# ScalarE issues the state space layer's row loads; its last group runs its steps in another order

## The chip, the cores and the metric

The kernel runs on one core of a Trainium2 chip. A core has five engines that work at the same time, each through its own list of instructions in a fixed order: TensorE (PE in the profile: matmuls and transposes), VectorE (DVE), ScalarE (ACT), GpSimd (POOL) and SyncE (SP). An instruction waits on semaphores for what it reads and for the buffer that it writes, and all that stands behind it on its engine waits with it. Transfers between the chip's memory and on-chip memory (DMA) are begun by an instruction of one of the engines and then run on 16 DMA engines; whoever needs the data waits for the landing. The metric is the time in microseconds (us) on the device.

## The reference

The program is a bidirectional encoder of two layers over 512 tokens of width 1024. Layer 0 mixes tokens with retention and neighbourhood attention, layer 1 with a state space mixer; each is followed by a gated feed-forward block with a short convolution, and all is normalised before and after. The change lies in the state space mixer:

```python
xbc = silu(depthwise_conv_centered(xbc, conv_w, conv_b))      # x, B, C of all groups
dt = softplus(dt_raw + dt_bias); log_a = dt * A               # per head and direction
# per group of 8 heads, chunks of 128 tokens:
seg = cs[:, :, None] - cs[:, None, :]                         # cs: running sums of log_a in a chunk
decay = exp(where(mask, seg, -inf))
y_intra = (q @ k^T * decay) @ v                               # within a chunk
y_inter = (q @ h) * exp(cs)                                   # from the state before the chunk
y = (y_fwd + y_bwd + x * d_skip) * silu(z)
yg = yg * rsqrt(mean(yg * yg) + EPS)                          # over the 512 channels of a group
out = (yg * norm_g) @ w_out
```

There are four groups of eight heads with 64 channels each. Every group has its own z, x, B and C projections (10 tiles of 128 channels) and its own 512 rows of `w_out`.

## The kernel before, in words

All large products are computed as three matmuls (`mm3`, L87 to L89): each operand is split into a rounded high part and a rest (`split`, L82 a cast on ACT, L83 a subtraction on DVE). A unit of weights (512 KB, `wst`) is loaded by SP, cast into `whi` on ACT, and its rest `wlo` made on DVE. So a matmul of 128x512 needs SP, ACT and DVE to have run ahead of PE.

`mixer1` is the state space mixer. It goes through the four groups, and for each through a string of steps, `SLOTS[g]`, which sets in which order the program is written; a scheduler then lays the instructions out per engine by their dependencies, priorities and free buffers. The steps are:

- `t6`: project tile 6 of this group, `n3`: project tile 3 of the next group (tile 0 is B, 1 is C, 2 to 5 are x, 6 to 9 are z). For tiles 0 to 5 a centred convolution of five taps follows (ACT L684, four DVE steps L687). `S` and `N`: SiLU of the waiting tiles of this or the next group (ACT, L693 and L696), and, for B and x, transposes on PE (L667) that ACT copies out (`bt`, `xt`, L668).
- `G`: the four products of C and B (`pg`, L712), copied to `gt` by ACT. `s0` to `s2`: the state after chunk 0 to 2 in both directions (PE `st` L723).
- `h3`: the decay matrix of head 3. Two rows of 512 running sums, one per direction, are loaded from the memory tensor `pd` and spread over all 128 partitions (tile `pb`, 256 KB each, L740, issued by SP). ACT adds a bias in eight pieces of 128x128 (L744), DVE merges the two directions (L746), ACT takes the exponential (`e`, L748), DVE multiplies by `gt` (L749).
- `i1`: the part of two heads (pair 1) that comes from the states: 6 PE products `pi` (L764), scaled on DVE by rows of `yd` that SP loads into `gain` (L756).
- `p1`: pair 1 itself: 8 PE products `py` from `e` and `xt` (L784), DVE adds `y` (L787) and multiplies by SiLU of z (L788), ACT squares (`sq`, L790), POOL adds the square to the sum of the group (L794), ACT and DVE split `y` into `yh` and `yl` (L796, L797).
- `r`: the mean of the squares by 4 products on PE (`pss`, L804), then DVE (L806) and POOL (`rg`, L808). `o0`, `o1`: the half-width output projections of the previous group (48 matmuls each), scaled by `rg` as they are added to `x`.

ACT needs a table for the exponential and another for SiLU; a change between them is an `ACT_TABLE_LOAD` row. After the last group the program (L889 to L899) multiplies its `y` by `w_out`: the two tiles of tokens 0 to 127 first (`first`), then `rms`, and then tile by tile the closing normalisation, and the norm and transposes (`pt`, L141) for the next block. All weights of that last projection are held at once, so that its eight halves need tiles from other tags: four from the states and four from `xt`.

Of the kernel before, what the change touches and what calls it, by code (L numbers as in the profile page):

```python
# [7 lines left out]
F32 = mybir.dt.float32  # L8
R32 = mybir.dt.float32r
BF16 = mybir.dt.bfloat16  # L10
U32 = mybir.dt.uint32
AF = mybir.ActivationFunctionType
ALU = mybir.AluOpType
# [3 lines left out]
P = 128  # L17
S = 512
NT = S // P
# [279 lines left out]
def mixer0(E, w0, w_v, w_fm, tabs, dist_d, logit, gn, bias, w_out, g_post_row, done):  # L299
# [235 lines left out]
NG = 4  # L535
HPG = 8
# [5 lines left out]
SLOTS = (  # L542
# [4 lines left out]
)  # L547


# [4 lines left out]
def mixer1(E, w_dt, w_fm, cw, dtc, cols, mask, w_out, g_post_row, done):  # L554
# [4 lines left out]
    nc, tc = E.nc, E.tc  # L559
    C = P  # L560
    H, H2 = SSD_H, 2 * SSD_H
    with ExitStack() as ctx:
        pool = lambda name, bufs: ctx.enter_context(tc.tile_pool(name=name, bufs=bufs))
        one, two, four = pool("m1", 1), pool("m1b", 2), pool("m1d", 4)
# [10 lines left out]
        mean = few.tile([P, 1], F32, name="mean")  # L575
# [9 lines left out]
        pd = E.dram.tile([H2, S], F32, name="pd")  # L585
# [84 lines left out]
        def project(o, i, ps=None):  # L670

            g = o["g"]
            if ps is None:
                w = E.wunit(w_fm[g, i])
                ps = E.mm.tile([P, S], F32, name="mm")
                E.proj_fm(ps, w)
            if i >= 6:
                r = four.tile([P, S], F32, name="z")
                o["silu"].append((r, ps, i))
                return  # L680
            r = (one if i == 0 else two if i == 1 else four).tile(
                [P, S], F32, name="bf" if i == 0 else "cf" if i == 1 else "xf")
            wc = lambda j: cwt[:, g, i, j:j + 1]
            nc.scalar.activation(r, ps, AF.Identity, scale=wc(2), bias=wc(5))  # L684
            for j, d in ((1, 1), (3, -1), (0, 2), (4, -2)):
                a, b = (slice(d, None), slice(0, S - d)) if d > 0 else (slice(0, S + d), slice(-d, None))
                nc.vector.scalar_tensor_tensor(r[:, a], ps[:, b], wc(j), r[:, a], op0=ALU.mult, op1=ALU.add)  # L687
            o["silu"].append((r, r, i))

        def silus(o):  # L690

            r, src, i = o["silu"][-1]
            lead = nc.scalar.activation(r, src, AF.Silu)  # L693
            with tc.issue_after(lead.ins):
                for r, src, _ in o["silu"][:-1]:
                    nc.scalar.activation(r, src, AF.Silu)  # L696
            for r, _, i in o["silu"]:
                o["t"][i] = r
                if i == 0:
                    o["bt"] = one.tile([P, NT, P], F32, name="bt")  # L700
                    to_tok(r, o["bt"])
                elif 2 <= i < 6:
                    if "x" not in o:
                        o["x"] = two.tile([P, NT, 512], F32, name="xt")
                    to_tok(r, o["x"][:, :, (i - 2) * P:(i - 1) * P])
            o["silu"] = []
# [9 lines left out]
        def state(o, dr, i):  # L716
# [14 lines left out]
                nc.vector.tensor_tensor(ns, ps, ns, op=ALU.add)  # L731
            o["st"][dr, i] = ns

        def head(o, j):

            g = o["g"]
            h = g * HPG + j
            pb = [three.tile([P, NT, C], F32, name="pb", bufs=5) for _ in range(2)]
            for dr in range(2):
                nc.sync.dma_start(pb[dr], pd[dr * H + h].partition_broadcast(P))  # L740

            for dr in range(2):
                for c in range(NT):
                    nc.scalar.activation(pb[dr][:, c], pb[dr][:, c], AF.Identity, scale=1.0 - 2 * dr,  # L744
                                         bias=tok[:, 0, c, dr * H + h:dr * H + h + 1])
            nc.vector.copy_predicated(pb[1], um.bitcast(U32).rearrange("p (o l) -> p o l", o=1).broadcast_to([P, NT, C]), pb[0])  # L746
            e = three.tile([P, NT, C], F32, name="e")
            nc.scalar.activation(e, pb[1], AF.Exp)  # L748
            o["m"][j] = e, nc.vector.tensor_tensor(e, e, o["gt"], op=ALU.mult)  # L749

        def inter(o, q):
# [24 lines left out]
        def pair(o, q):  # L776

            f = o["g"] * 4 + q
            y = o["yi"][q]
            py = E.px.tile([P, S], F32, name="py", tag="px")  # L780
            ms = [o["m"][2 * q + j] for j in range(2)]
            for c in range(NT):
                for j in range(2):
                    E.together([nc.tensor.matmul(py[j * 64:j * 64 + 64, c * C:(c + 1) * C],  # L784
                                                 o["x"][:, c, (2 * q + j) * 64:(2 * q + j + 1) * 64], ms[j][0][:, c],
                                                 start=True, stop=True)], [w for _, w in ms])
            nc.vector.tensor_tensor(y, py, y, op=ALU.add)  # L787
            nc.vector.tensor_tensor(y, y, o["t"][6 + q], op=ALU.mult)  # L788
            sq = (last if q == 0 else E.tmp).tile([P, S], F32, name="sq", tag="ssq" if q == 0 else "tmp")
            nc.scalar.activation(sq, y, AF.Square)  # L790
            if q == 0:
                o["sq"] = sq
            else:
                nc.gpsimd.tensor_tensor(o["sq"], o["sq"], sq, op=ALU.add)  # L794
            yh, yl = four.tile([P, S], R32, name="yh"), four.tile([P, S], R32, name="yl")
            nc.scalar.activation(yh, y, AF.Identity, scale=col[:, 1, f:f + 1])  # L796
            nc.vector.scalar_tensor_tensor(yl, y, col[:, 1, f:f + 1], yh.bitcast(F32), op0=ALU.mult, op1=ALU.subtract)  # L797
            o["y"].append((yh, yl))

        def rms(o):  # L800

            pss = E.px.tile([P, NT], F32, name="pss", tag="px")
            for c in range(NT):
                nc.tensor.matmul(pss[:, c:c + 1], o["sq"][:, c * C:(c + 1) * C], mean, start=True, stop=True)  # L804
            ss = few.tile([P, NT], F32, name="ss", bufs=2)
            nc.vector.tensor_scalar(ss, pss, EPS, None, op0=ALU.add)  # L806
            o["r"] = few.tile([P, NT], F32, name="rg", bufs=2)
            nc.gpsimd.tensor_tensor(o["r"], ss, E.mhalf.broadcast_to([P, NT]), op=ALU.pow)  # L808

        def out_mm(o, t, ws):  # L810
            ps = E.mm.tile([P, 512], F32, name="mm")
            tt = slice(t * P, (t + 1) * P)
            for k in range(4):
                yh, yl = o["y"][k]
                E.mm3(ps, yh[:, tt], yl[:, tt], *ws[k], k == 0, k == 3)
            return ps
# [19 lines left out]
            for t in range(NT):  # L836
                out_tile(o, n, t, ws)

        gs = [dict(g=g, t={}, st={}, m={}, yi={}, y=[], silu=[]) for g in range(NG)]
        def tiles(o, *ii):  # L840
            for i in ii:
                project(o, i)
            silus(o)

        w0 = [E.wunit(w_fm[0, i]) for i in range(3)]
        p0 = [E.mm.tile([P, S], F32, name="mm") for _ in range(3)]
# [6 lines left out]
            project(gs[0], i, p0[i])  # L853
        steps()
        three, ys, last = pool("m1e", 5), pool("m1y", 2), pool("m1f", 1)
        tiles(gs[0], 3)
        tiles(gs[0], 4, 5)
        for g, o in enumerate(gs):
            nx = gs[g + 1] if g + 1 < NG else None
            for step in SLOTS[g].split():  # L860
                a, i = step[0], int(step[1:] or 0)
# [22 lines left out]
        st = {}  # L884

        def fin(t, n, m):
            E.post_half(st, t, n, m, g_post, None, four.tile([P, 512], F32, name="mg", tag="z"))

        t4 = lambda pool, tags: [pool.tile([P, 512], R32, name="wo", tag=t) for t in tags]  # L889
        xt = two.tile([P, 4, 512], R32, name="wo", tag="xt")  # L890
        ws = [E.wunit(w_out[NG - 1, 0, 0]) + E.wunit(w_out[NG - 1, 0, 1]),
              E.wunit(w_out[NG - 1, 1, 0], t4(one, ("state00", "state10", "state01", "state11"))) + E.wunit(w_out[NG - 1, 1, 1], [xt[:, i] for i in range(4)])]
        first = [out_mm(gs[-1], 0, ws[n]) for n in range(2)]
        rms(gs[-1])
        for t in range(NT):
            for n in range(2):
# [5 lines left out]
def trunk(tc, x, norms, ab, ssd, ffns, out):  # L902

    nc = tc.nc
    with ExitStack() as ctx:
# [27 lines left out]
        mixer0(E, w0, *ab, norms[0, 1], then(norms[0, 2]))  # L933
        ffn(E, *ffns[0], norms[0, 3], then(norms[1, 0]))
        mixer1(E, *ssd, norms[1, 1], then(norms[1, 2]))
        ffn(E, *ffns[1], norms[1, 3], store)
        while E.late:
# [108 lines left out]
```

## Time and profile before

| | us |
|---|---|
| median of three runs | 1438.77 (1436.33 to 1439.25) |
| the profiled execution | 1439.13 |
| its span, first to last instruction | 1437.4 |
| PE busy in the span | 1400.4 (97%) |
| DVE busy | 914.4 (64%) |
| ACT busy | 707.1 (49%) |
| POOL busy | 61.1 (4%) |
| clock granted to TensorE, mean | 0.995 |

The profiled execution is 1.7 us longer than its span, and 0.36 us longer than the median. The state space mixer lies from about 655 to 1090 us of the span. A row of the timeline gives the start, the time that the row covers, engine, line, operation, tiles (written <- read), shapes, how many instructions the row holds, and in brackets how long the engine had been idle before it and what ended that. A PE matmul's own duration overlaps the next one's; what counts is the distance from start to start.

### The profile page before, as it was taken

The numbers are of one execution on the slowest core, as the hardware profiler recorded it, in microseconds if no ns is written. First come the engines' busy times: TensorE is split into PE (matmuls) and PEld (weight loads), VectorE is DVE, ScalarE is ACT, GpSimd is POOL, SyncE is SP. The second block draws the span as 40 slices with busy tenths as digits, with TensorE's granted clock in tenths as the row PEclk, the third lists the DMA queues.
The fourth block names the chain that finished last, engine by engine and source line by source line (L and its number), as shares of the span: only waits on it lengthen the run. The fifth ranks groups of instructions, "written<-read, shape, count | busy, mean of one in ns | idle before, by whom it ended". The sixth has DMA issues, their size and how long they took to land.

```text
span 1437.4 us, 17921 instructions
## 1 busy us (share of the span) xinstructions
PE 1400.4 (97%) x6830; PEld 1142.5 (79%) x6830; DVE 914.4 (64%) x1359; ACT 707.1 (49%) x1193; POOL 61.1 (4%) x67
## 2 busy tenths in 40 slices
PE   7999999999999999999999999989889999999998
PEld 6877777898888888888787777867678888888886
DVE  7478888665656552457887776976786566564242
ACT  5346666444444431424899676563444444443230
POOL 0010110100000000010001000010020000000000
PEclk9999999999999999999999999999999999999999
DMA  7443232223232332423575453452432322323231
GB/s 282 150 132 98 84 96 81 92 95 93 99 103 89 103 101 90 144 83 101 173 213 178 131 168 112 149 152 73 133 107 86 103 93 98 103 88 103 88 103 59
DMA packets 56949, 166.34 MB, mean 116 GB/s; under 512 B 7200, under 2 KB 7968, under 8 KB 56864
## 3 DMA queue, kind: packets, MB, share of 16 engines
q1 hardware_dynamic: 56864, 165.20, 35.7%
q8 instruction: 54, 0.88, 0.2%
q14 instruction: 31, 0.25, 0.1%
HBM read 157.57 MB, written 5.51 MB: 113 GB/s over the span
## 4 chain that ended last, share of the span: by engine, by line
PE 78%; DVE 8%; ACT 7%; DMA 4%; issue 2%; POOL 1%; SPq 0%; DVEq 0%; POOLq 0%; ACTq 0%
PE mm L87 24%; PE mm L89 23%; PE mm L88 23%; DMA pb<-pd 3%; ACT pb L744 2%; DVE wlo L83 1%; PE st L723 1%; ACT whi L82 1%; DVE xf L687 1%; PE pt L141 1%; PE y L450 1%; PE pi L764 1%; DVE yl L797 1%; PE sc L434 1%; PE sc L435 0%
## 5 line engine op out<-in xcount | busy, mean ns | idle before, releaser
L87 PE MATMUL mm<-xh,whi 128*128 128x512 f32 (+1 forms) x1216 | 465.6, 383 | 1.9 <-DVE xf L687 0.9
L89 PE MATMUL mm<-xl,whi 128*128 128x512 f32 (+2 forms) x1216 | 464.3, 382 | 3.0 <-DVE xl L83 3.0
L88 PE MATMUL mm<-xh,wlo 128*128 128x512 f32 (+2 forms) x1216 | 463.5, 381 | 0.0
L83 DVE TENSOR_TENSOR wlo<-wst,whi 128x1024 fp32r<-128x1024 f32 (+1 forms) x208 | 253.8, 1222 | 141.2 <-ACT whi L82 136.7
L82 ACT CAST whi<-wst 128x1024 fp32r<-128x1024 f32 (+1 forms) x208 | 216.5, 1042 | 154.0 <-PE mm L88 111.2
L87 PEld LDWEIGHTS mm<-xh,whi 128*128 128x128 f32 x1216 | 229.4, 189 | 47.7 <-issue 3.1
L89 PEld LDWEIGHTS mm<-xl,whi 128*128 128x128 f32 (+1 forms) x1216 | 229.5, 189 | 47.1 <-DVE xl L83 3.2
L88 PEld LDWEIGHTS mm<-xh,wlo 128*128 128x128 f32 (+1 forms) x1216 | 229.5, 189 | 42.7 <-issue 0.4
L228 DVE SCALAR_TENSOR_TENSOR cv<-mm,cwt,cv 128x511 f32<-128x511 f32 x88 | 66.0, 750 | 148.9 <-ACT cv L227 148.9
L227 ACT ACTIVATE cv<-mm,cwt 128x512 f32<-128x512 f32 x88 | 68.6, 780 | 127.9 <-PE mm L89 127.9
L87 PE MATMUL mm<-whi,hh 128*128 128x512 f32 x288 | 112.0, 389 | 0.0
L88 PE MATMUL mm<-whi,hl 128*128 128x512 f32 x288 | 112.0, 389 | 0.0
L89 PE MATMUL mm<-wlo,hh 128*128 128x512 f32 x288 | 112.0, 389 | 0.0
L744 ACT ACTIVATE pb<-pb,tok 128x128 f32<-128x128 f32 x256 | 81.4, 392 | 20.9 <-DMA pb<-pd 20.6
L82 ACT CAST hh<-cv 128x512 fp32r<-128x512 f32 x44 | 27.3, 621 | 103.4 <-DVE cv L236 103.4
L229 DVE SCALAR_TENSOR_TENSOR cv<-mm,cwt,cv 128x511 f32<-128x511 f32 x88 | 66.0, 750 | 3.0
L87 PEld LDWEIGHTS mm<-whi,hh 128*128 128x128 f32 x288 | 54.1, 188 | 11.3
L88 PEld LDWEIGHTS mm<-whi,hl 128*128 128x128 f32 x288 | 54.1, 188 | 11.2
L89 PEld LDWEIGHTS mm<-wlo,hh 128*128 128x128 f32 x288 | 54.1, 188 | 11.2
L687 DVE SCALAR_TENSOR_TENSOR xf<-mm,cwt,xf 128x511 f32<-128x511 f32 (+1 forms) x64 | 47.5, 744 | 11.5 <-ACT xf L684 11.1
L83 DVE TENSOR_TENSOR hl<-cv,hh 128x512 fp32r<-128x512 f32 x44 | 30.5, 693 | 28.9 <-ACT hh L82 28.9
L120 ACT ACTIVATE junk<-mm 128x512 bf16<-128x512 f32 x24 | 14.2, 593 | 66.1 <-PE mm L89 66.1
(235 smaller groups left out, 1878.1 us busy)
## 6 DMA issues: line engine op xcount, KB each, us to landing
wst<-in_f_up SPq DMA_DIRECT2D x88, 512.0 KB
wst<-in_f_down SPq DMA_DIRECT2D x44, 512.0 KB
wst<-in_c_fm SPq DMA_DIRECT2D x40, 512.0 KB
pb<-pd SPq DMA_DIRECT2D x64, 256.0 KB
wst<-in_ab_fm SPq DMA_DIRECT2D x20, 512.0 KB
gain<-yd SPq DMA_DIRECT2D x32, 256.0 KB
wst<-in_c_out SPq DMA_DIRECT2D x16, 512.0 KB
gain<-in_norms SPq DMA_DIRECT2D x8, 512.0 KB
```

The lines of the kernel that those rows point to most:

```text
L82: self.nc.scalar.copy(hi, src)
L83: self.nc.vector.tensor_tensor(lo, src, hi.bitcast(F32), op=ALU.subtract)
L87: mm(out, lh, rh, start=first, stop=False)
L88: mm(out, ll, rh, start=False, stop=False)
L89: mm(out, lh, rl, start=False, stop=last)
L141: nc.tensor.transpose(pt[:, j], xs[:, j * P:(j + 1) * P], self.ident)
L227: nc.scalar.activation(o, ps, AF.Identity, scale=w(1), bias=w(3))
L228: nc.vector.scalar_tensor_tensor(o[:, 1:], ps[:, :S - 1], w(0), o[:, 1:], op0=ALU.mult, op1=ALU.add)
L229: nc.vector.scalar_tensor_tensor(o[:, :S - 1], ps[:, 1:], w(2), o[:, :S - 1], op0=ALU.mult, op1=ALU.add)
L434: nc.tensor.matmul(ps, kt, qt[h], start=True, stop=False)
L687: nc.vector.scalar_tensor_tensor(r[:, a], ps[:, b], wc(j), r[:, a], op0=ALU.mult, op1=ALU.add)
L744: nc.scalar.activation(pb[dr][:, c], pb[dr][:, c], AF.Identity, scale=1.0 - 2 * dr, bias=tok[:, 0, c, dr * H + h:dr * H + h + 1])
```

## The change

Four things are edited, all in the state space mixer.

1. The row loads of the heads (`pb`) are issued by ACT instead of SP. A list holds the heads of all groups in the order of the strings; three heads are loaded ahead before group 0, and behind each exponential the next head's two loads are issued. `pb` has six buffers instead of five.
2. The string of the last group is rewritten: its gates and states stand at its head, the z tiles are spread, and the two halves of the previous group's output (`o0`, `o1`) stand among its pairs.
3. Pairs 0 and 1 of the last group write their split `y` to a tile of their own (`yx`, in the tag `xt`); the last half-unit of `w_out` takes two `yh` and two `yl` tiles for it.
4. The last pair of the last group no longer goes through POOL's sum: `rms` multiplies the sum of the first three squares and the fourth square separately, adding up in PE's accumulator: 8 products instead of 4. All of them wait for the third sum's and the fourth square's producers.

```diff
 SLOTS = (
...
-    "t9 G h0 s0 s1 o0 t8 h4 s2 h2 i0 t6 o1 t7 S h1 h3 p0 i1 p1 i2 i3 h5 p2 h6 h7 p3",
+    "G h0 s0 s1 t9 h1 t8 s2 i0 t6 S h2 t7 p0 i1 S h3 o0 p1 i2 h4 h5 o1 p2 i3 h6 h7 p3",
 )
...
+        heads = [g * HPG + int(a[1:]) for g in range(NG) for a in SLOTS[g].split() if a[0] == "h"]
+        pbs = []
+
+        def load():
+            if heads:
+                h = heads.pop(0)
+                pbs.append([three.tile([P, NT, C], F32, name="pb", bufs=6) for _ in range(2)])
+                for dr in range(2):
+                    nc.scalar.dma_start(pbs[-1][dr], pd[dr * H + h].partition_broadcast(P))
 
         def head(o, j):
-            pb = [three.tile([P, NT, C], F32, name="pb", bufs=5) for _ in range(2)]
-            for dr in range(2):
-                nc.sync.dma_start(pb[dr], pd[dr * H + h].partition_broadcast(P))
+            pb = pbs.pop(0)
...
             nc.scalar.activation(e, pb[1], AF.Exp)
+            load()
             o["m"][j] = e, nc.vector.tensor_tensor(e, e, o["gt"], op=ALU.mult)
...
-            nc.scalar.activation(sq, y, AF.Square)
+            w = nc.scalar.activation(sq, y, AF.Square)
             if q == 0:
-                o["sq"] = sq
+                o["sq"] = [sq]
+            elif q == 3 and o["g"] == NG - 1:
+                o["sq"].append(sq)
             else:
-                nc.gpsimd.tensor_tensor(o["sq"], o["sq"], sq, op=ALU.add)
-            yh, yl = four.tile([P, S], R32, name="yh"), four.tile([P, S], R32, name="yl")
+                w = nc.gpsimd.tensor_tensor(o["sq"][0], o["sq"][0], sq, op=ALU.add)
+            o["sqw"].append(w)
+            if o["g"] == NG - 1 and q < 2:
+                if q == 0:
+                    o["yx"] = two.tile([P, 4, S], R32, name="yx", tag="xt")
+                yh, yl = o["yx"][:, 2 * q], o["yx"][:, 2 * q + 1]
+            else:
+                yh, yl = four.tile([P, S], R32, name="yh"), four.tile([P, S], R32, name="yl")
...
             for c in range(NT):
-                nc.tensor.matmul(pss[:, c:c + 1], o["sq"][:, c * C:(c + 1) * C], mean, start=True, stop=True)
+                for i, sq in enumerate(o["sq"]):
+                    E.together([nc.tensor.matmul(pss[:, c:c + 1], sq[:, c * C:(c + 1) * C], mean, start=i == 0,
+                                                 stop=sq is o["sq"][-1])], o["sqw"][2:])
...
         three, ys, last = pool("m1e", 5), pool("m1y", 2), pool("m1f", 1)
+        for _ in range(3):
+            load()
...
-        xt = two.tile([P, 4, 512], R32, name="wo", tag="xt")
         ws = [E.wunit(w_out[NG - 1, 0, 0]) + E.wunit(w_out[NG - 1, 0, 1]),
-              E.wunit(w_out[NG - 1, 1, 0], t4(one, ("state00", "state10", "state01", "state11"))) + E.wunit(w_out[NG - 1, 1, 1], [xt[:, i] for i in range(4)])]
+              E.wunit(w_out[NG - 1, 1, 0], t4(one, ("state00", "state10", "state01", "state11"))) + E.wunit(w_out[NG - 1, 1, 1], t4(four, ("yh", "yh", "yl", "yl")))]
```

The lines below are the order of instructions on one engine: line, operation, tile written <- read, size, and how many in a row. In the changed kernel the lines of `mixer1` behind the edit are numbered higher: the bias is L754, the exponential L758, `py` L795, `sq` L801, `yh` L815, and L744 is the row load on ACT.

**ACT at the head of group 0.** Before, from the gate copy on (behind these rows come one more exponential, one bias piece, a table load and the four SiLUs of z):

```order
L714 COPY gt<-pg 128x512
L744 ACTIVATE pb<-pb,tok 128x128 x6
L726 COPY state_5699<-st 128x512
L744 ACTIVATE pb<-pb,tok 128x128
L726 COPY state_5705<-st 128x512
L744 ACTIVATE pb<-pb,tok 128x128 x13
L748 ACT_TABLE_LOAD
L748 ACTIVATE e<-pb 128x512 x2
L82 CAST whi<-wst 128x1024
L744 ACTIVATE pb<-pb,tok 128x128 x10
```

In the changed kernel, from the last bias pieces ahead of the first exponential:

```order
L754 ACTIVATE pb<-pb,tok 128x128 x14
L82 CAST whi<-wst 128x1024 x2
L758 ACT_TABLE_LOAD
L758 ACTIVATE e<-pb 128x512
L744 DMA pb<-pd 128x512 x2
L693 ACT_TABLE_LOAD
L693 ACTIVATE z<-mm 128x512
L696 ACTIVATE z<-mm 128x512 x3
L758 ACT_TABLE_LOAD
L758 ACTIVATE e<-pb 128x512
L744 DMA pb<-pd 128x512 x2
L758 ACTIVATE e<-pb 128x512
```

The exponentials of heads 0 and 1 stood together behind one table load. Now the four SiLUs of z stand between them, with a table load on either side, and 24 bias pieces instead of 20 stand before the first.

**ACT at the end of group 2,** around the square of its last pair (`sq`). Before:

```order
L748 ACTIVATE e<-pb 128x512 x2
L744 ACTIVATE pb<-pb,tok 128x128 x14
L684 ACTIVATE xf<-mm,cwt 128x512
L82 CAST whi<-wst 128x1024
L790 ACTIVATE sq<-y 128x512
L796 ACTIVATE yh<-y,col 128x512
```

In the changed kernel:

```order
L758 ACTIVATE e<-pb 128x512 x2
L744 DMA pb<-pd 128x512 x2
L754 ACTIVATE pb<-pb,tok 128x128 x10
L684 ACTIVATE xf<-mm,cwt 128x512
L801 ACTIVATE sq<-y 128x512
L815 ACTIVATE yh<-y,col 128x512
```

Four fewer bias pieces (they belong to heads of group 3) stand ahead of the square, the cast stands behind it, and two loads are issued in between.

**PE at the end of the last group.** Before, with the last of the state products of pair 3:

```order
L764 MATMUL pi<-cf,state_8337 128x128
L784 MATMUL py<-e,xt 64x128 x16
L87 MATMUL mm<-whi,yh 128x512
L87 MATMUL mm<-wo,yh 128x512
L87 MATMUL mm<-whi,yh 128x512
```

In the changed kernel:

```order
L795 MATMUL py<-e,xt 64x128 x8
L775 MATMUL pi<-cf,state_8168 128x128
L775 MATMUL pi<-cf,state_8180 128x128
L775 MATMUL pi<-cf,state_8274 128x128
L775 MATMUL pi<-cf,state_8174 128x128
L775 MATMUL pi<-cf,state_8187 128x128
L775 MATMUL pi<-cf,state_8281 128x128
L795 MATMUL py<-e,xt 64x128 x8
L87 MATMUL mm<-whi,yx 128x512
L88 MATMUL mm<-whi,yx 128x512
```

Pairs 2 and 3 stood together, and 36 matmuls of the last output projection followed up to the first product `pss`. Now the state products of pair 3 stand between the two pairs, and 30 matmuls, most of which read pairs 0 and 1 (`yx`), follow up to `pss`.

More of the change, by code (lines that the diff above doesn't have):

```diff
@@ L837, in out @@
                 out_tile(o, n, t, ws)
-        gs = [dict(g=g, t={}, st={}, m={}, yi={}, y=[], silu=[]) for g in range(NG)]
+        gs = [dict(g=g, t={}, st={}, m={}, yi={}, y=[], silu=[], sqw=[]) for g in range(NG)]
         def tiles(o, *ii):
```

## The prediction

> **What bounds the kernel now.** I read the head of the page first, then the waits of PE within the state space mixer (655 to 1090 us), then the timelines where the large waits fall.
>
> ```profile
> span 1437.4 us, 17921 instructions
> PE 1400.4 (97%) x6830; PEld 1142.5 (79%) x6830; DVE 914.4 (64%) x1359; ACT 707.1 (49%) x1193; POOL 61.1 (4%) x67
> ```
>
> PE is busy for all but 37 us of the span. The change takes no large product away, so it can give only PE's idle time in this mixer and the clock that is lost behind it. That idle time, by what ended it (total, times, longest):
>
> ```profile
> PE pss L804 <- POOL sq L794: 6.2, 3, 5.3
> PE mm L89 <- DVE xl L83: 3.0, 1, 3.0
> PE pt L141 <- DVE xs L132: 2.3, 3, 1.5
> PE py L784 <- DVE ti L768: 1.7, 2, 1.3
> PE mm L87 <- ACT yh L796: 1.4, 2, 0.7
> PE mm L88 <- DVE yl L797: 1.0, 1, 1.0
> PE mm L87 <- DVE xf L687: 0.9, 1, 0.9
> PE mm L87 <- ACT z L693: 0.7, 1, 0.7
> PE pt L667 <- ACT bf L696: 0.3, 1, 0.3
> ```
>
> These rows sum to 17.5 us. The largest stall, 5.3 us, is at the end of group 2; I call it A. The rows `py`, `yh`, `yl` and one short wait for `pss` are the end of the last group (B); `xl` and `xs` are the tail behind it.
>
> **Part 1, stall A.** PE ran dry at 959.5 and went on at 964.9:
>
> ```profile
> 959.05 0.39 PE L87 MATMUL mm<-xh,whi 128*128 128x512 f32 x1
> 959.28 0.39 PE L88 MATMUL mm<-xh,wlo 128*128 128x512 f32 x1
> 964.93 1.82 PE L804 MATMUL pss<-mean,sq 128*128 128x1 f32 x8 [5.26 <-POOL sq L794]
> ```
>
> POOL's sum needs the square, the square needs `y`, and ACT is where the time goes:
>
> ```profile
> 956.83 1.28 ACT L744 ACTIVATE pb<-pb,tok 128x128 f32<-128x128 f32 x4 [1.28 <-DMA pb<-pd]
> 959.63 1.27 ACT L744 ACTIVATE pb<-pb,tok 128x128 f32<-128x128 f32 x4 [1.51 <-DMA pb<-pd]
> 960.81 0.76 ACT L684 ACTIVATE xf<-mm,cwt 128x512 f32<-128x512 f32 x1
> 962.40 0.63 ACT L790 ACTIVATE sq<-y 128x512 f32<-128x512 f32 x1
> ```
>
> ```profile
> 957.41 0.70 DVE L788 TENSOR_TENSOR y<-y,z 128x512 f32<-128x512 f32 x1
> ```
>
> ```profile
> 963.17 1.70 POOL L794 TENSOR_TENSOR sq<-sq 128x512 f32<-128x512 f32 x1 [19.72 <-ACT sq L790]
> ```
>
> `y` was there at 958.1, but the square began at 962.4: in front of it ACT stood waiting for row loads of the next group (1.28 and 1.51 us), then did their bias, a convolution and a cast. The stall has a second price: the granted clock (PEclk, the column behind POOL).
>
> ```profile
> 960.00:970.00 10.00, 5.07 (x16) 4.39 (x17) 6.39 (x8) 3.65 (x8) 2.72 (x2) 0.75 0.33 101
> 970.00:980.00 10.00, 10.00 (x53) 8.23 (x52) 3.74 (x7) 7.68 (x12) 0.00 (x0) 0.91 0.18 52
> ```
>
> A clock of 0.75 and of 0.91 over 10 us each loses 2.5 + 0.9 = 3.4 us. Whoever removes A gains up to 8.7 us.
>
> In the changed order the last four bias pieces and the cast are gone from before the square, and the loads were issued at least one exponential earlier, so nothing there waits for a landing. The square can start about 0.7 us (the convolution) behind `y`; square 0.6 and sum 1.3 to 1.7 follow. Against this PE has 34 matmuls as cover from the end of `py` where it had 38, 4 x 0.23 = 0.9 us less. The sum is then ready at 958.1 + 0.7 + 0.6 + 1.7 = 961.1 on the old clock, and PE comes at 959.5 − 0.9 = 958.6, 2.5 us earlier. Two things shorten that: DVE has one merge of a later head less before `y` (a step of the size of the `y` row, 0.7), and the convolution waits for PE alone and so may run before `y` is there (0.7). I take 1.0 us left of the stall, bounds 0 and 2.5, and full clock. **Gain 5.3 + 3.4 − 1.0 = 7.7 us** (6.2 to 8.7).
>
> **Part 2, a new stall at the first pair of group 0.** This is the price of moving the loads: the order there changed, though the string did not. Before:
>
> ```profile
> 701.79 1.09 ACT L668 COPY xt<-pt 128x512 f32<-128x512 f32 x2
> 711.90 1.28 ACT L748 ACT_TABLE_LOAD   x1
> 713.19 1.15 ACT L748 ACTIVATE e<-pb 128x512 f32<-128x512 f32 x2
> 714.25 1.04 ACT L82 CAST whi<-wst 128x1024 fp32r<-128x1024 f32 x1
> 720.54 1.28 ACT L693 ACT_TABLE_LOAD   x1
> 721.84 0.60 ACT L693 ACTIVATE z<-mm 128x512 f32<-128x512 f32 x1
> 722.33 1.58 ACT L696 ACTIVATE z<-mm 128x512 f32<-128x512 f32 x3
> ```
>
> ```profile
> 701.03 1.09 PE L667 MATMUL pt<-head,xf 128*128 128x128 f32 x8
> 719.15 1.09 PE L784 MATMUL py<-e,xt 128*64 128x128 f32 x16
> ```
>
> ```profile
> 715.51 0.68 DVE L749 TENSOR_TENSOR e<-e,gt 128x512 f32<-128x512 f32 x1
> ```
>
> Both exponentials were over at 714.3 and their products with the gate at 716.2, three us before PE wanted them at 719.15, so `py` waited for nothing. Now:
>
> - PE puts 34 matmuls where 13 stood ahead of the second transposes of x: 21 x 0.23 = 4.8 us later, 705.8, and the first copy can start at 706.3.
> - From those copies to the table load ACT took 711.9 − 701.8 = 10.1 us, with 1.1 us of waiting in it. One more bias piece (1.28 / 4 = 0.3 us) stands there now: 9.3 us, to 715.6. The six loads issued ahead lie before the copies, where ACT waits for PE anyway.
> - Two casts (1.04 each, pipelined 0.94): 717.5. Table 1.28, exponential of head 0 0.5: 719.3. Two loads issued, 0.3 to 0.7 each (below): 720.0. Table 1.28 and four SiLUs (0.5 + 1.6): 723.4. Table, exponential of head 1, product with the gate (0.6): 725.8.
> - PE has 10 matmuls more before `py` (2.3 us) and arrives at 719.15 + 2.3 = 721.4.
>
> So `py` waits 4.4 us. It cannot be under 2.5: the SiLU waits for a matmul that PE ends at 719.3, and 2.1 + 1.3 + 0.5 + 0.6 follow, to 723.9. It is 6 if the first load lands late and holds the copies. Nothing covers it: behind `py` in PE's order stand the state products and all later matmuls. To it belongs a clock loss. The only other pair of idle time and clock loss in this mixer is the tail, where 3.0 us of waiting (`xl` above) was followed by
>
> ```profile
> 1060.00:1070.00 10.00, 5.50 (x32) 4.89 (x33) 9.05 (x16) 4.46 (x12) 2.34 (x3) 0.87 0.32 109
> 1070.00:1080.00 10.00, 9.64 (x77) 9.27 (x77) 7.76 (x14) 6.25 (x11) 1.08 (x2) 0.96 0.46 165
> ```
>
> that is 1.3 + 0.4 = 1.7 us. Between 1.7 for 3.0 us and 3.4 for 5.3 us I take 2.7 for 4.4 us. **Loss 4.4 + 2.7 = 7.1 us** (2.5 to 9.4).
>
> [...]
>
> **Part 3, the rest of groups 0 and 1 on ACT.** Windows of 10 us from 690 to 790 (columns PE, PEld, DVE, ACT, POOL), ACT's bias rows in them, and the loads that SP issued in them (shortest, median, longest ns; 33 of 64):
>
> ```profile
> sum 100.00, PE 98.25 PEld 78.01 DVE 79.95 ACT 93.52 POOL 5.31; mean PE 9.82 PEld 7.80 DVE 8.00 ACT 9.35 POOL 0.53
> L744 ACT ACTIVATE pb<-pb,tok 128x128 f32<-128x128 f32 x125 | 39.6, 391 | 5.3 <-DMA pb<-pd 5.1
> L740 SPq DMA_DIRECT2D pb<-pd x33: 319/325/2083, 698.6 to 787.0; - x33
> 711.89 2.97 SPq L740 DMA_DIRECT2D pb<-pd  x4
> ```
>
> ACT is full in this stretch. It has 6.5 us free, 5.1 of them waits for row loads. About 33 issues come to it: 10.7 us at the median 0.32, up to 24 at the 0.74 of a loaded queue. What an issue costs on ACT no row shows; I take 0.35, 11.6 us. Free for it are the 6.5 us and the 4.4 us that PE loses at the first pair anyway, together 10.9; the last 0.7 us fall behind 790, where ACT has room. So I put no second stall here, with 0 to 13 us for the range. SP loses 64 issues and gains nothing that PE waits for, since no wait of PE above ends on a weight's landing.
>
> **Part 4, B and the tail.** Pairs 2 and 3 came back to back, so that PE waited for each step of them: 1.7 + 1.4 + 1.0 and 0.6 at `pss` = 4.7 us. Now 30 matmuls (6.8 us), most on pairs 0 and 1, lie between `py` of pair 3 and `pss`, and pair 2 has 2.5 us more ahead of it. DVE's steps for the two pairs and the weights' rests between them sum to about 6.5 us, so they end about when PE gets there. What is added is four products of `pss`:
>
> ```profile
> 1043.44 0.61 PE L804 MATMUL pss<-mean,sq 128*128 128x1 f32 x4 [0.57 <-POOL sq L794]
> 1044.46 0.50 PE L804 MATMUL pss<-mean,sq 128*128 128x1 f32 x4
> ```
>
> Each row of four records is two products, 0.5 and 0.4 us to the next matmul: 0.8 us for four more. The square now goes to PE without POOL's 1.3 us. On DVE the step behind `pss` stands ahead of the last `yl` and two rests, which I count as 0.6 us of new waiting. **Gain 4.7 − 0.8 − 0.6 = 3.3 us** (1 to 4.5). The same three DVE steps delay the first output tile by 1.7 us while six more matmuls (1.4 us) and the longer `pss` cover its chain: of the tail's 5.3 us I count **0.5 us** gained (−1 to 3). The small waits of the list (`xf`, `z`, `bf`, and the third of `pss`, 2.3 us) lie at places that the new order moves: **1.5 us** (0 to 2.3).
>
> **The sum:** 7.7 − 7.1 + 3.3 + 0.5 + 1.5 = 5.9 us less. From the profiled execution 1439.13 − 5.9 = 1433.2; the median of the runs shown is 0.36 lower, so I forecast **1433 us**.
>
> **Rivals.**
>
> *ACT becomes the bound of groups 0 and 1 (slower).* If an issue costs ACT 0.6 us, the 33 take 20 us, 9 more than is free; PE then waits at every pair of the two groups, and each wait over about 3 us costs clock. At 9 + 3 us the time is 1445. It decides from about 0.5 us an issue: 16.5 − 10.9 = 5.6 us eats the gain. For it: ACT at 93.5%, and rows of SP up to 2.08 us. Against it: the median row of 0.32.
>
> [...]
>
> *A larger gain.* The first pair waits its floor of 2.5 us without loss of clock (+4.6), and A goes wholly (+1.0): 1427.4.
>
> **Chances.** My forecast 0.48, ACT as bound 0.20, no wait removed 0.12, larger gain 0.20. A measurement of this kernel tells about 0.2% (2.9 us) from no change, so faster is below 1435.9 and slower above 1441.6. Faster: 0.42 of the forecast's 0.48 and the larger gain's 0.20. Same: 0.05 of the forecast, 0.10 of the unremoved wait, 0.06 of ACT as bound with a cheaper issue. The rest, 0.17, is slower. The forecast's own range is 1428 to 1438; that of 8 in 10 reaches into both sides, 1424 to 1444.
>
> **What would show it.** Right, if the wait `pss <- POOL sq` of 5.3 us at the end of group 2 is at most 2 and the clock there stays 1.00; if `py` of group 0's first pair has an idle time of 3 to 6 us that ends on the exponential's product, with a clock under 1.00 behind it; if no row of `yh`, `yl` or `py` at the end of the last group exceeds 0.7. Wrong, if that first pair does not wait (then 1427), if ACT's waits of PE appear all through 720 to 800 (then the first rival), or if ACT still waits for row loads ahead of the square.

## The result: 11 us faster

| | median, us | range, us | ratio to before, 95% interval |
|---|---|---|---|
| before | 1437.55 | 1435.44 to 1439.25 | |
| changed | 1426.35 | 1424.27 to 1428.27 | 0.9922 (0.9909 to 0.9934) |

The change gains 0.8%. The forecast of 1433 had the sign and most of the places. The wide range of 1424 to 1444 held the time, but the forecast's own range of 1428 to 1438 did not: the gain of 11.2 us is nearly twice the 5.9 us that I had added up. The profiled execution of the changed kernel has a span of 1425.2 us against 1437.4. 1.0 of these 12.2 us lies ahead of the state space mixer, in code that the change does not touch: the first transposes behind the mixer's step sizes start at 692.8 instead of 693.8. In the other versions below they start between 692.5 and 696.3, so 1 us is within the spread of single executions.

PE's waits between 650 and 1085 us in the changed kernel (total, times, longest) answer to the list of before:

```profile
PE mm L89 <- DVE xl L83: 3.0, 1, 3.0
PE mm L87 <- ACT z L693: 2.0, 1, 2.0
PE pt L141 <- DVE xs L132: 1.1, 1, 1.1
PE py L795 <- DVE e L760: 0.7, 1, 0.7
PE pss L824 <- POOL sq L807: 0.6, 1, 0.6
```

The 5.3 us at the end of group 2 are 0.6, and all waits of the last group (`py`, `yh`, `yl`) are gone. The wait for `z` has grown from 0.7 to 2.0 and a `py` wait of 0.7 is new, both at the first pair of group 0. The windows in which the clock or the idle time moved (columns PE, PEld, DVE, ACT, POOL, then the granted clock):

```profile
720.00:730.00 10.00, 9.29 (x46) 7.49 (x45) 6.09 (x10) 6.17 (x13) 0.00 (x0) 0.66 0.70 247
960.00:970.00 10.00, 9.54 (x57) 8.39 (x58) 4.67 (x9) 8.31 (x18) 1.42 (x2) 1.00 0.35 99
1030.00:1040.00 10.00, 10.00 (x39) 7.73 (x39) 8.70 (x16) 2.09 (x5) 2.02 (x2) 0.83 0.45 157
1050.00:1060.00 10.00, 6.99 (x43) 6.55 (x43) 8.39 (x15) 3.58 (x9) 2.92 (x3) 0.83 0.49 158
```

At A (960 to 970) the clock is full again. It is lost at three other places: 3.4 us behind the new stall, 1.7 us behind the last `pss`, and 1.7 us in the tail, as before.

How ScalarE fared at the head of group 0 (the rows marked ACTq are its queue issuing loads, the others its arithmetic):

```profile
697.51 4.58 ACTq L744 DMA_DIRECT2D pb<-pd  x3
702.13 0.59 ACT L668 COPY bt<-pt 128x512 f32<-128x512 f32 x1 [4.14 <-DMA pb<-pd]
713.79 1.99 ACT L82 CAST whi<-wst 128x1024 fp32r<-128x1024 f32 x2
714.97 0.33 ACTq L744 DMA_DIRECT2D pb<-pd  x1
717.74 1.28 ACT L693 ACT_TABLE_LOAD   x1
719.04 0.60 ACT L693 ACTIVATE z<-mm 128x512 f32<-128x512 f32 x1
721.12 1.28 ACT L758 ACT_TABLE_LOAD   x1
```

```profile
719.69 0.50 PE L87 MATMUL mm<-xh,whi 128*128 128x512 f32 x1 [2.04 <-ACT z L693]
723.82 1.98 PE L795 MATMUL py<-e,xt 128*64 128x128 f32 x16 [0.71 <-DVE e L760]
1028.45 1.92 PE L824 MATMUL pss<-mean,sq 128*128 128x1 f32 x16
```

The second row of ACTq holds three issues. Its last two are the fifth and the sixth of the six that go ahead:

```profile
698.35 1.25 ACTq L744 DMA_DIRECT2D pb<-pd  x1
701.76 0.33 ACTq L744 DMA_DIRECT2D pb<-pd  x1
```

Two things are to be seen. The fifth issue takes 1.25 us by itself, the sixth begins only 2.2 us later, when the first load has landed, and ScalarE's arithmetic stands idle for 4.1 us behind the six. And a load that is issued later, at 714.97, takes its 0.33 us inside a cast that runs from 713.8 to 715.8: this issue runs beside ScalarE's arithmetic. All 64 issues together take 23.1 us, and arithmetic runs during 17.0 of them.

### The profile page after: what moved, and what is told of

Read it like the earlier page. It is cut to its first block, busy times and chain, and to the rows that moved or that the text cites. A ratio compares the mean times of both kernels' runs of the same rounds, so it can differ in the third digit from the quotient of the medians.

```text
span 1425.2 us, 17860 instructions
## 1 busy us (share of the span) xinstructions
PE 1398.7 (98%) x6838; PEld 1143.5 (80%) x6838; DVE 909.0 (64%) x1359; ACT 706.9 (50%) x1192; POOL 61.1 (4%) x66
## 4 chain that ended last, share of the span: by engine, by line
PE 91%; ACT 3%; DVE 3%; issue 1%; DMA 1%; POOL 0%; DVEq 0%; SPq 0%; POOLq 0%; ACTq 0%
PE mm L87 27%; PE mm L88 27%; PE mm L89 27%; PE pi L775 2%; PE st L723 1%; PE py L795 1%; PE y L450 1%; PE pt L141 1%; PE pt L667 1%; PE sc L434 1%; PE sc L435 0%; DMA x<-in_x 0%; PE pt L502 0%; PE y L512 0%; PE sc L485 0%
## 5 line engine op out<-in xcount | busy, mean ns | idle before, releaser
L754 ACT ACTIVATE pb<-pb,tok 128x128 f32<-128x128 f32 x256 | 79.6, 392 | 5.5 <-DMA pb<-pd 2.8
L87 PEld LDWEIGHTS mm<-whi,hh 128*128 128x128 f32 x288 | 54.1, 188 | 11.2
L89 PEld LDWEIGHTS mm<-wlo,hh 128*128 128x128 f32 x288 | 54.1, 188 | 11.2
```

The lines of the kernel that those rows point to most:

```text
L87: mm(out, lh, rh, start=first, stop=False)
L89: mm(out, lh, rl, start=False, stop=last)
```

## The experiments

The theory after the result: the moved loads take A away and make the new stall; the last group's string takes away the waits of the last group; the eight products of `pss` cost clock. The rival: the string alone does it, and the moved loads are worth nothing. All ratios are to the runs of before that were taken beside them. Beside string_only, first_sp and best the median of before was 1439.39, beside the others 1437.4 to 1437.7, so that these three are better compared with the others by their ratios.

| kernel | median, us | ratio to before (95%) |
|---|---|---|
| loads_only: edit 1 | 1431.96 | 0.9963 (0.9950 to 0.9975) |
| group_only: edits 2 to 4 | 1426.66 | 0.9920 (0.9894 to 0.9945) |
| string_only: edit 2 | 1427.88 | 0.9923 (0.9906 to 0.9941) |
| sp_ahead: all, loads issued by SyncE | 1430.20 | 0.9942 (0.9922 to 0.9962) |
| pool_sum: all but edit 4 | 1426.60 | 0.9919 (0.9896 to 0.9942) |
| s_later: all, SiLUs later | 1425.26 | 0.9909 (0.9893 to 0.9926) |
| pss_r32: all, `pss` in one pass | 1422.49 | 0.9889 (0.9875 to 0.9902) |
| group_r32: group_only, `pss` in one pass | 1423.04 | 0.9899 (0.9884 to 0.9914) |
| pss_all: all, 8 products in each group | 1429.59 (one run) | |
| first_sp: all, SyncE issues the first three heads | 1423.72 | 0.9895 (0.9877 to 0.9913) |
| best: first_sp and `pss` in one pass | 1420.13 | 0.9877 (0.9858 to 0.9897) |

**Each half alone.** loads_only is the changed kernel with the old string, tiles and sum of the last group (the tiles of `w_out` go back as well, as shown under string_only):

```diff
-    "G h0 s0 s1 t9 h1 t8 s2 i0 t6 S h2 t7 p0 i1 S h3 o0 p1 i2 h4 h5 o1 p2 i3 h6 h7 p3",
+    "t9 G h0 s0 s1 o0 t8 h4 s2 h2 i0 t6 o1 t7 S h1 h3 p0 i1 p1 i2 i3 h5 p2 h6 h7 p3",
...
-            elif q == 3 and o["g"] == NG - 1:
-                o["sq"].append(sq)
...
-            if o["g"] == NG - 1 and q < 2:
+            if False:
```

> Edit 1 alone: ScalarE issues the row loads three heads ahead, the last group stays as before. Theory (the loads remove stall A, 8.1 us, and make the stall at the first pair, 6.2 us with its clock; the end of the last group keeps its 4.7 us of waits): pss at the end of group 2 waits under 1.5 us, clock 1.00 there, time about 1434 us. Rival (A went because the new string of the last group takes other heads' bias steps from in front of the square): A stays at about 5 us, time about 1442 us.

group_only gives the loads back to `head`:

```diff
-            pb = pbs.pop(0)
+            pb = [three.tile([P, NT, C], F32, name="pb", bufs=5) for _ in range(2)]
+            for dr in range(2):
+                nc.sync.dma_start(pb[dr], pd[dr * H + h].partition_broadcast(P))
...
-            load()
...
-        for _ in range(3):
-            load()
```

> Edits 2 to 4 alone: SyncE issues the row loads as before, the last group is new. Theory: no stall at the first pair of group 0, A stays (5.3 us idle and 3.4 us of clock), the end of the last group loses 4.7 us of waits and pays 0.9 us for the products and 1.7 us of clock: about 1434.5 us. Rival (A went by the string): A goes too, about 1426 us or less.

Edit 1 alone gains 5 us, edits 2 to 4 alone 11 us, all four together 11 us: the two halves don't add up. PE's waits of loads_only show A gone and the last group as it was:

```profile
PE pt L141 <- DVE xs L132: 2.2, 3, 1.5
PE mm L87 <- ACT z L693: 2.0, 1, 2.0
PE py L795 <- DVE ti L779: 1.7, 2, 1.3
PE mm L87 <- ACT yh L813: 1.4, 2, 0.7
PE pss L822 <- POOL sq L805: 1.1, 2, 0.6
```

But in group_only A is gone too, with the loads where they were. Its waits of PE, ScalarE's wait for row loads in the mixer (of before, then of group_only), and ScalarE's rows at the end of group 2:

```profile
PE pss L825 <- POOL sq L808: 0.8, 1, 0.8
PE mm L87 <- DVE xf L687: 0.6, 1, 0.6
PE mm L87 <- ACT z L693: 0.5, 1, 0.5
```

```profile
ACT pb L744 <- DMA pb<-pd: 20.6, 20, 3.1
ACT pb L756 <- DMA pb<-pd: 16.7, 17, 3.0
```

```profile
957.15 0.78 ACT L684 ACTIVATE xf<-mm,cwt 128x512 f32<-128x512 f32 x1 [0.28 <-PE mm L89]
957.83 0.62 ACT L802 ACTIVATE sq<-y 128x512 f32<-128x512 f32 x1
958.35 0.71 ACT L816 ACTIVATE yh<-y,col 128x512 fp32r<-128x512 f32 x1
960.18 1.28 ACT L756 ACTIVATE pb<-pb,tok 128x128 f32<-128x128 f32 x4 [0.19 <-DMA pb<-pd]
962.01 1.28 ACT L756 ACTIVATE pb<-pb,tok 128x128 f32<-128x128 f32 x4 [0.56 <-DMA pb<-pd]
```

ScalarE still waits 16.7 us for row loads, but the bias pieces that wait (960.2 and 962.0) stand behind the square now. So A has two remedies, either is enough, and together they remove it once. The theory of loads_only held: the loads do remove A. The theory of group_only, that A stays without them, fell, and its rival held. That the loads also bring the new stall is confirmed: `z` costs 0.5 us in group_only and 2.0 in loads_only.

**The string without its tiles.**

```diff
-            if o["g"] == NG - 1 and q < 2:
+            if False:
...
+        xt = two.tile([P, 4, 512], R32, name="wo", tag="xt")
         ws = [E.wunit(w_out[NG - 1, 0, 0]) + E.wunit(w_out[NG - 1, 0, 1]),
-              E.wunit(w_out[NG - 1, 1, 0], t4(one, ("state00", "state10", "state01", "state11"))) + E.wunit(w_out[NG - 1, 1, 1], t4(four, ("yh", "yh", "yl", "yl")))]
+              E.wunit(w_out[NG - 1, 1, 0], t4(one, ("state00", "state10", "state01", "state11"))) + E.wunit(w_out[NG - 1, 1, 1], [xt[:, i] for i in range(4)])]
```

(from group_only, and without the separate fourth square)

> Edit 2 alone: the last group's new string, with row loads by SyncE, no tiles of their own for pairs 0 and 1 and one sum of squares. Theory (the own tiles are what the string needs: with o0 and o1 among the pairs, the previous group's yh and yl are still read while pairs 0 and 1 want their buffers, and DVE and ScalarE stand behind those writes): A goes, but PE waits 3 us or more among the pairs of the last group: 1430 to 1436 us. Rival (the buffers come free in time): as with edits 2 to 4, about 1427 us.

1427.9 us. Its ratio, 0.9923, lies within the interval of group_only. PE's waits on `pss` are 2.6 us in all in place of 0.8, on `z` 1.3 in place of 0.5, and on `yl` only 0.2: the buffers come free in time, and the theory of the tiles fell. Edits 3 and 4 buy nothing that can be measured here.

**Who issues, and how far ahead.**

```diff
-                    nc.scalar.dma_start(pbs[-1][dr], pd[dr * H + h].partition_broadcast(P))
+                    nc.sync.dma_start(pbs[-1][dr], pd[dr * H + h].partition_broadcast(P))
```

> The changed kernel with the same loads, as far ahead, issued by SyncE instead of ScalarE. Theory (the lead of three heads and the six buffers matter, not who issues): within 2 us of the changed kernel, 1426 us, A gone. Rival (SyncE's own waits for weight buffers hold the row loads back): ScalarE waits for row loads by 10 us and more in the mixer again, A returns, about 1435 us.

1430.2 us lies between the two. ScalarE's wait for row loads, PE's wait at A and the clock there:

```profile
ACT pb L754 <- DMA pb<-pd: 15.1, 13, 3.3
PE pss L824 <- POOL sq L807: 1.2, 1, 1.2
960.00:970.00 10.00, 10.00 (x45) 8.00 (x45) 3.23 (x6) 5.84 (x9) 1.02 (x1) 0.83 0.25 75
```

ScalarE waits for row loads by 15.1 us, as the rival said, where the changed kernel has 2.8 and the 4.1 of the six issues. So it does matter who issues: with SyncE the lead that the program asks for does not come about. From the end of an issue to the first bias step on its tile it is 6.2 us in the median, against 10.6 in the changed kernel and 5.5 in group_only. But A does not return as the rival had it: it costs 1.2 us of waiting and 1.7 us of clock. That it stays this small I put down to the new string, which this version shares with group_only (0.8 us there; the matmuls behind it start 0.23 us apart, against 0.43 at the clock of 0.50 in the changed kernel's drop at 1031.7); no separate run shows it. The first pair of group 0 has no stall, as in group_only. The profiled execution was the fastest of its five; what the others lost, 2.2 to 4.5 us more, no trace shows. Whether this version is really slower than group_only, which also issues from SyncE, stays open: the intervals overlap.

**The last pss.** The clock falls to 0.83 at 1030 to 1040 us in the changed kernel although PE never waits there; 1.8 us of `pss` products, each one column wide, stand just ahead.

pool_sum: edit 4 undone.

```diff
-            elif q == 3 and o["g"] == NG - 1:
-                o["sq"].append(sq)
```

> The changed kernel without edit 4: the last square goes through GpSimd's sum and pss has 4 products again. Theory (the 1.8 us of products of 128x1 make the throttle lower the clock at 1031 to 1035 us): no clock under 1.00 there, which gives 1.7 us, the products 0.9 us less, the wait for GpSimd's sum 1.5 us more: about 1425 us. Rival (the drop has another cause): the clock drops there all the same, about 1427 us.

pss_all: the same separate square in every group.

```diff
-            elif q == 3 and o["g"] == NG - 1:
+            elif q == 3:
```

> The changed kernel with the fourth square multiplied separately in all four groups, so that each pss has 8 products (16 records, 1.8 us) in place of 4. Theory (1.8 us of products of one column lower the clock): the clock drops behind each of the four pss, at about 789, 881, 962 and 1031 us, by 1.7 us each. Rival: it drops in the last group alone.

pss_r32: squares, sums and the mean's constant in the rounded format, so that a product is one record in place of two (8 in 0.95 us here, 16 in 1.92 in the changed kernel); the squares lose their low bits.

```diff
-        mean = few.tile([P, 1], F32, name="mean")
-        nc.vector.memset(mean, 1.0 / 512)
+        mean0 = few.tile([P, 1], F32, name="mean0")
+        nc.vector.memset(mean0, 1.0 / 512)
+        mean = few.tile([P, 2], R32, name="mean")
+        nc.vector.tensor_copy(mean, mean0.broadcast_to([P, 2]))
...
-            sq = (last if q == 0 else E.tmp).tile([P, S], F32, name="sq", tag="ssq" if q == 0 else "tmp")
+            sq = (last if q == 0 else E.tmp).tile([P, S], R32, name="sq", tag="ssq" if q == 0 else "tmp")
...
-            pss = E.px.tile([P, NT], F32, name="pss", tag="px")
+            pss = E.px.tile([P, NT, 2], F32, name="pss", tag="px")
```

> The changed kernel with the squares, their sums and the constant of the mean kept in the rounded format of the other matmuls (the squares lose their low bits), so that the 8 products of pss are one pass each, about 0.9 us in place of 1.8. Theory (the throttle goes by how long the array does next to nothing, 1.8 us of products of one column count as idle): no clock under 1.00 at 1030 to 1036 us; 1.7 us of clock and 0.9 us of products gained, less what the tail waits in place of them: 1424 us. Rival (the drop hangs on something else there): clock 0.83 again, 1425.5 us.

group_r32: the same on group_only.

> The same products in one pass, with the row loads issued by SyncE as before the change. Theory (moving the loads buys nothing once the last group's string is new, and costs the stall at the first pair, 6.2 us, of which other waits in groups 0 to 2 give back 3 to 4): 2 to 3 us faster than the same with ScalarE's loads, 1421.5 us. Rival (both edits are worth the same together as the string alone): equal to it within 1 us.

pool_sum has the time of the changed kernel, 1426.60 us against 1426.35, which is nearer to its rival's 1427 than to the theory's 1425: four products and a longer wait for GpSimd's sum (1.1 us) fill the same stretch. pss_all refutes the simple theory: 16 records at each of its four `pss`, at about 789, 881, 962 and 1032 us, and a clock of 1.00 in all the windows below, of which those from 960 and from 1030 hold the third and the fourth `pss` and what follows them; the other two end too early for that.

```profile
780.00:790.00 10.00, 10.00 (x59) 8.09 (x58) 8.68 (x12) 7.62 (x17) 0.00 (x0) 1.00 0.56 163
870.00:880.00 10.00, 10.00 (x66) 8.19 (x66) 6.50 (x10) 9.32 (x17) 0.00 (x0) 1.00 0.42 130
960.00:970.00 10.00, 10.00 (x54) 8.41 (x53) 7.17 (x12) 5.95 (x12) 1.02 (x1) 1.00 0.65 190
1030.00:1040.00 10.00, 10.00 (x53) 8.07 (x52) 7.23 (x13) 3.72 (x8) 2.02 (x2) 1.00 0.44 154
```

The same holds for the first pair in that run: 3.6 us idle between 720 and 730, and a clock of 1.00. So a drop is not a matter of the stretch alone; the section on the hardware comes back to this. pss_r32 is 3.9 us faster than the changed kernel. Its products are half as many records, and the clock stays at 1.00 there:

```profile
1026.32 0.95 PE L826 MATMUL pss<-mean,sq 128*128 128x2 f32 x8
```

That makes 0.9 + 1.7 us; the other 1.3 no row names. Elsewhere in the mixer that profile loses 1.7 us of clock less at the first pair and 1.7 more in the tail, which cancel. The gain holds on both bases: group_r32 is 3.6 us faster than group_only. That the two are equal, 1422.5 and 1423.0, confirms the rival of group_r32: with the new string, ScalarE's loads are worth nothing, and cost nothing that the medians show.

**The new stall.** s_later moves the SiLUs of group 0's z behind both exponentials:

```diff
-    "G s0 s1 t6 t7 s2 i0 h0 t8 t9 S h1 p0 i1 n0 h2 h4 h3 p1 i2 n6 n1 h5 n7 i3 n9 p2 N n3 n4 n2 n5 h6 h7 p3 n8 r N",
+    "G s0 s1 t6 t7 s2 i0 h0 h1 t8 t9 S p0 i1 n0 h2 h4 h3 p1 i2 n6 n1 h5 n7 i3 n9 p2 N n3 n4 n2 n5 h6 h7 p3 n8 r N",
```

> The changed kernel with group 0's string reading h0 h1 t8 t9 S p0 in place of h0 t8 t9 S h1 p0, so that ScalarE takes both exponentials before the four SiLUs and PE has 6 matmuls ahead of py in place of 16. Theory (the stall at the first pair is the detour over two table loads and four SiLUs, and it costs 2.75 us of waits and 3.4 us of clock): py waits about 1.2 us, no wait for z, clock 1.00 from 720 to 730, about 5 us faster than the changed kernel: 1421 us. Rival (ScalarE has too much work there, whatever its order): the wait moves to another matmul or to the second pair, time within 2 us of 1426.

The order came out as meant, and the wait for `z` went, but `py` waited 2.7 us in its place and 1.7 us of clock were still lost. The time, 1425.3 us, is the rival's.

```profile
723.14 1.53 PE L795 MATMUL py<-e,xt 128*64 128x128 f32 x16 [2.71 <-DVE e L760]
```

ScalarE's rows show that it was late from the start:

```profile
698.85 6.21 ACTq L744 DMA_DIRECT2D pb<-pd  x3
705.11 0.59 ACT L668 COPY bt<-pt 128x512 f32<-128x512 f32 x1 [5.77 <-DMA pb<-pd]
```

The hold behind the six issues was 5.8 us in this run, 1.6 more than in the changed kernel's profile; the fifth issue took 2.74 us here and 1.25 there. So the hold itself was the next suspect. first_sp lets SyncE issue the first three heads' loads:

```diff
-        def load():
+        def load(eng=nc.scalar):
...
-                    nc.scalar.dma_start(pbs[-1][dr], pd[dr * H + h].partition_broadcast(P))
+                    eng.dma_start(pbs[-1][dr], pd[dr * H + h].partition_broadcast(P))
...
         for _ in range(3):
-            load()
+            load(nc.sync)
```

> The changed kernel with both exponentials ahead of the SiLUs as in s_later, and the first three heads' loads issued by SyncE; ScalarE issues the other 29 heads'. Theory (ScalarE's sixth load waits for the first one's landing and holds ScalarE 4 to 6 us at 698 to 704; that made py wait 2.7 us there): no hold, py of the first pair waits at most 1.2 us, clock 1.00 from 720 to 730: 1422 us. Rival (the bias steps ahead of the first exponential set it, not the hold): py waits 2 us or more, 1425 us.

The stall is gone, in waits and in clock:

```profile
721.87 1.09 PE L795 MATMUL py<-e,xt 128*64 128x128 f32 x16
```

```profile
720.00:730.00 10.00, 10.00 (x62) 8.28 (x61) 7.13 (x13) 7.03 (x16) 0.00 (x0) 1.00 0.93 302
```

1423.7 us against 1426.35; by the ratios 0.9895 against 0.9922, with intervals that still overlap a little. It keeps s_later's string, but that plays no part: with the first loads on SyncE, the old string and the new one give the same order on every engine. What had set the order that I read in the changed kernel, with 34 matmuls ahead of the second transposes and the SiLUs between the exponentials, was the place of six load issues on ScalarE; with them on SyncE it is 13 again. So first_sp takes away the hold and the other order at once, and does not show how much each of them cost.

**Both together**, first_sp with the edit of pss_r32, is the fastest version of the study:

> first_sp with the one-pass products of pss_r32 (squares in the rounded format). Theory: the two gains add, 3 to 4 us under first_sp: 1418.5 us. Rival: the end of the last group waits for something else, no more than 1 us under first_sp.

```profile
PE mm L89 <- DVE xl L83: 3.0, 1, 3.0
PE pt L141 <- DVE xs L132: 1.3, 1, 1.3
PE pss L826 <- POOL sq L809: 0.8, 1, 0.8
PE st L725 <- DVE xs L723: 0.7, 1, 0.7
```

1420.1 us, 3.6 under first_sp: the two gains add. Most of what is left of waiting in the mixer is the tail, with 4.3 us, and 3.4 us of clock behind it in this profile.

## Why the prediction was right, and where its terms were off

The direction was right, but only in part for the reasons given. The prediction counted A as the gain of the moved loads and let the new string earn the end of the last group alone; the runs show that the string removes A by itself and that the loads add nothing to it. The sum came out on the right side because A was counted once, whoever removed it. The measured time lies nearest to the rival of a larger gain, 1427.4, but its condition of a first pair without loss of clock did not come, so that this nearness is luck.

| term | predicted, us | measured in the profiles, us |
|---|---|---|
| A | −7.7 | −8.1 (5.3 − 0.6 idle, 3.4 clock) |
| first pair of group 0 | +7.1 | +6.2 (2.04 + 0.71 idle, 3.4 clock) |
| rest of groups 0 and 1 on ScalarE | 0 | 0 |
| end of the last group | −3.3 | −2.0 (4.7 idle gone but 0.1; products +0.9, clock +1.7) |
| tail | −0.5 | −1.0 (5.3 to 4.3 idle, clock the same) |
| small waits | −1.5 | −2.1 |
| sum | −5.9 | −7.0 |

- **A** was right in size. Its cause was right in the row (ScalarE waits for row loads ahead of the square) and half wrong in the remedy: I gave the gain to the fewer pieces and to the earlier loads as one thing, and did not see that the new string alone does it too.
- **The new stall** was found in the order and on the right engine, with its clock. The step that failed is where PE waits: I had it at `py`, and it stopped 10 matmuls earlier, at the one that needs a buffer which the SiLU of z frees. While ScalarE went on to the second exponential, PE did those matmuls, so that 2.75 us were idle and not 4.4. Idle time of half the size cost more clock (3.4) than the 2.7 that I had interpolated from the length of the wait; that way of pricing is wrong.
- "The six loads issued ahead lie before the copies, where ACT waits for PE anyway" was the step with the wrong idea: the six hold ScalarE's copies for 4 to 6 us, a case that stood there only for the upper bound. first_sp, where SyncE issues them, is 2.6 us faster.
- **ScalarE's 11.6 us of issues** were priced as if they took the place of its arithmetic. Most do not: arithmetic runs during 17.0 of the 23.1 us of all issues. Between 690 and 790 us, where I had called ScalarE full (93.5 us of 100), it is busy for 79.9 in the changed kernel, and PE's only waits over 0.2 us there are at the first pair. The first rival, priced on the issues, did not come.
- **The end of the last group**: all waits went, as worked out. The term missing was the clock behind `pss`.
- **No wait removed**, 0.12 in the chances, did not come: A went, and ScalarE's waits for row loads are 20.6 us before, 2.8 and 4.1 in the changed kernel, and 15.1 where SyncE issues the same list. That the move is nevertheless worth nothing beside the new string has this reason: at A, where PE felt them, the string alone takes the waits from in front of the square.

The sum of these rows is 7.0 us, and the same two landmarks of the program, the transposes at 692.8 and the first matmul on `hh` in the next block, have come 11.1 us closer. About 1.8 us of the rest lie in the waits too: the matmul ahead of a wait counts as busy for its whole 0.39 us, though the next one otherwise starts 0.23 us after it, and between the landmarks PE runs dry 9 times in place of 21. The other 2 us no row names, and they stay open; the runs of the changed kernel alone lie 4.0 us apart.

## What to carry to other kernels

Before adding up two edits, ask whether they remove the same wait: here each alone brought the 5.3 us down to under 1, and together they did no more. Most issues of a load on ScalarE ran beside its arithmetic (17.0 of 23.1 us), but where one took long or had to wait for an earlier load's landing, all of the engine's later work stood behind it (4.1 us at the first six); so look where the first loads of a series are issued. And the clock can fall where PE has not waited: behind 1.8 us of products of one column (the last `pss`) it read 0.83 over 1030 to 1040 us in the changed kernel, and 1.00 in s_later, first_sp and pss_all; so such a stretch is to be watched when a long chain of work hangs on the clock.

## What the runs showed of the hardware

**Where the clock fell.** The granted clock in windows of 0.1 us in the changed kernel, at the three places where it fell in the mixer:

```profile
721.00:721.10 0.10, 0.10 (x2) 0.10 (x1) 0.10 (x1) 0.10 (x1) 0.00 (x0) 1.00 1.69 451
721.10:721.20 0.10, 0.10 (x2) 0.04 (x1) 0.10 (x1) 0.08 (x2) 0.00 (x0) 0.68 0.48 143
1031.60:1031.70 0.10, 0.10 (x2) 0.00 (x0) 0.10 (x1) 0.00 (x0) 0.10 (x1) 1.00 0.00 0
1031.70:1031.80 0.10, 0.10 (x2) 0.00 (x0) 0.10 (x2) 0.00 (x0) 0.10 (x1) 0.74 0.00 0
1055.50:1055.60 0.10, 0.10 (x4) 0.10 (x3) 0.10 (x1) 0.10 (x3) 0.10 (x1) 1.00 0.20 82
1055.60:1055.70 0.10, 0.10 (x3) 0.10 (x2) 0.10 (x1) 0.10 (x2) 0.10 (x1) 0.71 0.40 164
```

The clock in the low stretches is 0.50. They last 6.8 us from 721.1, and 3.4 us from 1031.7 and from 1055.6; half of that is lost, 3.4 and twice 1.7 us. In before it is 0.50 for 6.8 us from 965.0 and for 3.4 us from 1067.4.

What stood ahead of them, with the start of what PE did next in brackets:

| profile | clock falls at | ahead of it | clock lost, us |
|---|---|---|---|
| before | 965.0 | 5.3 us idle (964.9) | 3.4 |
| before | 1067.4 | 1.5 us idle (1061.4), 3.0 us idle (1066.5) | 1.7 |
| changed | 721.1 | 2.0 us idle (719.7); 0.7 us more inside the stretch (723.8) | 3.4 |
| changed | 1031.7 | 1.8 us of `pss` products (1030.2) | 1.7 |
| changed | 1055.6 | 1.1 us idle (1049.4), 3.0 us idle (1054.4) | 1.7 |

So 2.0 us of idle time, with 0.7 us inside the stretch, cost as much as 5.3 and more than 3.0, while in pss_all the window from 720 to 730 has 3.6 us of it and a clock of 1.00. The length of a wait alone does not give the price. What does, no run here shows, and neither do they show why the clock fell behind the last `pss` of the changed kernel (0.83 over 1030 to 1040 us) and not in s_later, first_sp and pss_all, where PE does the same products (1.00 over the same 10 us).

For whoever reads one profile this means that 1.7 or 3.4 us of it can be luck, ahead of the mixer too: group_only's profile lost 1.7 us of clock at 90 us, in code that no kernel here changes.
